# Squared relu of two MLPs: the square moved from VectorE to ScalarE

## The chip, the core and the metric

One core of a Trainium2 chip runs the whole kernel in one launch. The metric is the time of that launch on the device, in microseconds (us). Three timed runs of the kernel before gave 1197.14, 1199.34 and 1201.36 us; the median is 1199.34 us. The change is judged by the median of the changed kernel's runs against this.

## What is computed

A sequence of 256 tokens of width 1024 goes through two blocks, all in float32. The first block has two layers, each of attention and an MLP with a squared relu; the second has a SwiGLU layer, a hybrid mixer and a second SwiGLU layer, all three modulated by vectors that come from a condition. The change touches the two MLPs of the first block alone:

```python
D_MODEL, SEQ, D_FF = 1024, 256, 4 * 1024

def squared_relu_mlp(x, w_up, w_down):
    return jnp.square(jax.nn.relu(x @ w_up)) @ w_down

for layer in range(2):
    ...
    h = h + squared_relu_mlp(rms_norm(h, mlp_norm[layer]), w_up[layer], w_down[layer])
```

## The kernel before, in words

**Products in three parts.** Every float32 operand of a large product is split into a high part, rounded to the type fp32r, and a low part, the rest. Each product is three matmuls: high by high, high by low, low by high (`part`, lines 212 to 214, where tokens are the rows of the result; `by_feature`, lines 245 to 247, where features are). So every piece of a weight needs two instructions before TensorE can use it: ScalarE writes the high part `wh` (`prepare`, line 174, or line 178 where a gain is multiplied in) and VectorE the low part `wl` (line 175 or 179; for a few pieces GpSimd at line 175).

**Weights as a stream.** A list (`plan`) holds all pieces of 512 KB, called slabs, in the order of use. SyncE's queue loads them (line 147) into a ring of five buffers `raw` (RB = 5); a load can start when the slab five places ahead of it has been read by its last reader. The prepared parts lie in rings of five (WB = 5), freed by TensorE. `take` prepares up to two slabs beyond the one that is asked for. Between the slabs of the MLPs stand slabs of the modulation weights `w_ada`, about one for every two: these are not multiplied on TensorE, but by VectorE (`ada_step`, line 485, two instructions for a slab), and GpSimd adds the result up over the partitions (line 490) after every fourth slab.

**One MLP.** `hidden` runs over eight blocks of 512 hidden features (`MLP_CUTS`). For block j TensorE first makes the up product of block j (`by_feature`, 96 matmuls of 256 columns, into two tiles of PSUM), and then the down product of block j - 1 (`by_token`, 48 matmuls of 512 columns, accumulated in four tiles). I call these two an up pass and a down pass, and both together a round. Between the passes stands, in program order, the hidden part of block j (`up` in `mlp`, lines 836 to 840). It handles two tiles, and for each there are four instructions: ScalarE's relu (line 837, from PSUM), VectorE's product of relu and input (line 839, tile `sq`), ScalarE's high part `mh` of the square (line 259) and VectorE's low part `ml` (line 260). Their results are first used by TensorE one up pass later.

**Order.** The schedule is written by hand: each engine executes its instructions in the order in which the program lists them, and waits for semaphores where an operand comes from another engine. So a relu of the second tile stands on ScalarE's queue behind the high part of the first tile's square, which waits for VectorE. In the second MLP some rounds also hold VectorE instructions for the modulation (`modulation`, line 507), which wait for a small load of a gain row.

The tile `sq` is taken from a ring of six buffers (tag `rb`), the relu's tile from a ring of three (tag `ra`).

Of the kernel before, what the change touches and what calls it, by code (L numbers as in the profile page):

```python
# [12 lines left out]
AF = mybir.ActivationFunctionType  # L13
OP = mybir.AluOpType
# [14 lines left out]
def kernel(ctx: ExitStack, tc: tile.TileContext, a: dict, out: bass.AP):  # L29
    nc = tc.nc  # L30
    PE, ACT, DVE, POOL = nc.tensor, nc.scalar, nc.vector, nc.gpsimd
# [23 lines left out]
    def mm_ps(shape=(TP, 512)):  # L55
        return psm.tile(list(shape), F32, tag="mm", name="mm")
# [3 lines left out]
    def sb(tag, shape=(TP, 512), dt=F32, name=None):  # L60
        return s2.tile(list(shape), dt, tag=tag, name=name or tag, bufs=BUFS[tag])
# [4 lines left out]
    def tt(shape, name="t", dt=F32):  # L66
        return tiny.tile(list(shape), dt, tag="t", name=name)
# [7 lines left out]
    def cols(s):  # L75
        return slice(s * 512, (s + 1) * 512)
# [21 lines left out]
    def finish(*some):  # L98

        while any(s in sides for s in some):  # L100
            for s in some:
                if s in sides:
                    advance(s)
# [129 lines left out]
    def by_feature(idx, xT, ps, before=None):  # L233

        k = 0
        for i in idx:
            if before is not None:
                before(k)
            for wh, wl in take(i):
                xh, xl = (z[:, k % 4, :] for z in xT[k // 4])  # L240
                for n in range(2 * len(ps)):
                    c = slice(n * TP, (n + 1) * TP)
                    o = ps[n // 2][:, n % 2, :]

                    PE.matmul(o, lhsT=wh[:, c], rhs=xh, start=k == 0 and n % 2 == 0, stop=False)  # L245
                    PE.matmul(o, lhsT=wh[:, c], rhs=xl, start=False, stop=False)  # L246
                    PE.matmul(o, lhsT=wl[:, c], rhs=xh, start=False, stop=k == 7 and n % 2 == 1)  # L247
                k += 1
                if k % 2:
                    tick()  # L250
            done(i)
            tick()
# [33 lines left out]
    def hidden_part(q):  # L286

        hi, lo = pair("m", (TP, 2, S))
        split(hi, lo, q)
        return [(hi[:, j, :], lo[:, j, :]) for j in range(2)]  # L290
# [506 lines left out]
    def hidden(plans, cuts, up, update, order=None, tail=None):  # L797


        acc = [[None, None], [None, None]]  # L800
        made = None
        ups, downs = plans
        for j in range(len(cuts) + 1):
            new = up(j, ups[j]) if j < len(cuts) else None
            if j == 1:
                acc = [[acc_ps() for _ in range(2)] for _ in range(2)]
            if 0 < j < len(cuts):
                for s in range(2):
                    apart = tail is not None and j == len(cuts) - 1 and s == 1
                    by_token(downs[j - 1][s], by_block(made), [acc[t][s] for t in range(2)], first=j == 1,  # L810
                             last=(lambda t, n: t == 1 and n == len(downs[j - 1][s]) - 1) if apart else False)
            elif j == len(cuts):
                if tail is not None:
                    update(1, 1, acc[1][1])
                token_first(downs[j - 1], by_block(made), acc, False, lambda t, s: update(t, s, acc[t][s]),
                            order, tail)
            made = new

    def mlp(layer, plans, xT, vs, chains, next_chain, between=lambda j: None, order=BY_HALF):
        r2 = [None, None]  # L820

        def up(j, ids):
            between(j)
            ps = [mm_ps((TP, 2, S)) for _ in range(2)]

            def before(k):
                if j == 0:
                    finish(chains[0][k // 4], chains[1][k // 4])
            by_feature(ids[0], xT, ps, before)
            if j == 0:  # L830
                for t in range(2):
                    r2[t] = tt((TP, 1), "r2")
                    DVE.reciprocal(r2[t], vs[t][0])
            hT = []
            for p in ps:
                r = sb("ra", (TP, 2, S), name="relu")
                ACT.activation(out=r, in_=p, func=AF.Relu)
                q = sb("rb", (TP, 2, S), name="sq")
                DVE.tensor_tensor(q, r, p, op=OP.mult)
                hT += hidden_part(q)  # L840
            return hT

        def update(t, s, p):
            DVE.scalar_tensor_tensor(out=h[t][:, cols(s)], in0=p, scalar=r2[t], in1=h[t][:, cols(s)],
                                     op0=OP.mult, op1=OP.add)
            next_chain(t, s)
        hidden(plans, MLP_CUTS, up, update, order)
# [747 lines left out]
```

## Time and profile before

| what | value |
|---|---|
| timed runs | 1197.14, 1199.34, 1201.36 us; median 1199.34 us |
| the profiled execution | 1202.77 us, its span 1201.1 us |
| mean granted clock of TensorE | 0.991 |
| TensorE matmuls busy | 1163.7 us, 97% |
| VectorE busy | 847.7 us, 71% |
| ScalarE busy | 652.0 us, 54% |
| GpSimd busy | 301.3 us, 25% |
| read from memory | 240.65 MB, 201 GB/s over the span |
| the square on VectorE, line 839 | 32 instructions, 21.8 us |

The profile is of one execution, and all durations below come from it. Its own time is 1.67 us more than its span, and 3.43 us more than the median of the timed runs. Matmuls are pipelined, and the page models their ends: TensorE counts as busy from a matmul's start to its modelled end, so the idle time that a view gives is shorter than the delay between two starts. PE stands for TensorE's matmuls, PEld for its weight loads, DVE for VectorE, ACT for ScalarE, POOL for GpSimd, SP for SyncE; L839 is line 839.

### The profile page before, as it was taken

Reading aid. Unit: us, or ns where it says so; the run is one execution under the profiler, and the core shown is the slowest. Engines: PE = TensorE matmul, PEld = TensorE weight load, DVE = VectorE, ACT = ScalarE, POOL = GpSimd, SP = SyncE. Lnnn points to the kernel's source line nnn. Section 1 sums busy time; section 2 is a strip of 40 time slices with the busy share of each in tenths; the row PEclk is TensorE's granted clock in tenths of the full one; section 3 lists DMA queues with packets and bytes.
Section 4 is the critical chain, followed back from the end, with each engine's and each line's share of the span. In section 5 each row is a group of like instructions: output and inputs, shape, how many; then the busy total and the mean of one; then the engine's idle time right before and its main releaser. Section 6 shows DMA issues by size and latency. Waiting matters only on the chain.

```text
span 1201.1 us, 19954 instructions
## 1 busy us (share of the span) xinstructions
PE 1163.7 (97%) x7669; PEld 1051.3 (88%) x7669; DVE 847.7 (71%) x1188; ACT 652.0 (54%) x1115; POOL 301.3 (25%) x260
## 2 busy tenths in 40 slices
PE   8999999999999999999989999999999999999997
PEld 7987989988899799889868999979987887899996
DVE  5664688887676478788767888756776767666445
ACT  6476664555546664555654444545766563444443
POOL 3044202222002601112063121154147314112002
PEclk9999999999999999999989999999999999999999
DMA  8643567886653448789737888853733363877660
GB/s 274 188 140 107 178 218 253 282 272 215 193 171 119 137 147 277 244 283 308 252 121 248 298 278 303 292 163 101 222 90 104 104 225 110 272 222 244 209 192 36
DMA packets 128479, 243.04 MB, mean 202 GB/s; under 512 B 8515, under 2 KB 16612, under 8 KB 128384
## 3 DMA queue, kind: packets, MB, share of 16 engines
q1 hardware_dynamic: 126688, 239.96, 61.0%
q0 software_dynamic: 1376, 1.28, 0.5%
q8 instruction: 60, 0.98, 0.3%
q10 hardware_dynamic: 320, 0.53, 0.1%
q14 instruction: 35, 0.29, 0.1%
HBM read 240.65 MB, written 1.09 MB: 201 GB/s over the span
## 4 chain that ended last, share of the span: by engine, by line
PE 65%; DVE 16%; DMA 7%; ACT 6%; issue 4%; POOL 2%; SPq 0%; POOLq 0%; DVEq 0%; ACTq 0%
PE mm L247 8%; PE mm L246 8%; PE mm L245 8%; PE acc L212 8%; PE acc L213 7%; PE acc L214 7%; DVE wl L179 4%; DMA raw<-in_w_down_dram 4%; PE acc L245 3%; PE acc L247 3%; PE acc L246 3%; DVE wl L175 3%; ACT wh L174 2%; DVE ada L485 2%; PE mm L212 2%
## 5 line engine op out<-in xcount | busy, mean ns | idle before, releaser
L174 ACT CAST wh<-raw 128x1024 fp32r<-128x1024 f32 (+1 forms) x231 | 237.4, 1042 | 222.0 <-DMA raw<-in_w_down_dram 72.4
L175 DVE TENSOR_TENSOR wl<-raw,wh 128x1024 fp32r<-128x1024 f32 (+1 forms) x193 | 261.0, 1368 | 135.1 <-ACT wh L174 132.1
L247 PE MATMUL mm<-xh,wl 128*128 128x256 f32 x1088 | 308.6, 284 | 5.1 <-DVE wl L179 5.1
L245 PE MATMUL mm<-xh,wh 128*128 128x256 f32 x1088 | 308.5, 284 | 0.0
L246 PE MATMUL mm<-xl,wh 128*128 128x256 f32 x1088 | 307.8, 283 | 0.0
L179 DVE SCALAR_TENSOR_TENSOR wl<-raw,cols,wh 128x512 fp32r<-128x512 f32 (+1 forms) x270 | 204.1, 807 | 68.2 <-ACT wh L178 68.2
L247 PEld LDWEIGHTS mm<-xh,wl 128*128 128x128 f32 x1088 | 208.7, 192 | 6.4 <-DVE wl L179 6.3
L178 ACT ACTIVATE wh<-raw,cols 128x512 fp32r<-128x512 f32 (+1 forms) x270 | 175.9, 708 | 64.9 <-PE acc L246 20.4
L246 PEld LDWEIGHTS mm<-xl,wh 128*128 128x128 f32 x1088 | 208.7, 192 | 0.8
L245 PEld LDWEIGHTS mm<-xh,wh 128*128 128x128 f32 x1088 | 208.7, 192 | 0.8
L212 PE MATMUL acc<-wh,mh 128*128 128x512 f32 x524 | 207.4, 396 | 0.0
L213 PE MATMUL acc<-wl,mh 128*128 128x512 f32 x524 | 205.2, 392 | 0.5 <-DVE wl L175 0.5
L214 PE MATMUL acc<-wh,ml 128*128 128x512 f32 x524 | 205.0, 391 | 0.0
L490 POOL PARTITION_ALL_REDUCE ada<-ada x18 | 64.9, 3608 | 352.0 <-DVE ada L485 143.1
L175 POOL TENSOR_TENSOR wl<-raw,wh 128x1024 fp32r<-128x1024 f32 (+1 forms) x38 | 91.5, 2410 | 130.8 <-ACT wh L174 125.6
L214 PEld LDWEIGHTS acc<-wh,ml 128*128 128x128 f32 x524 | 98.8, 189 | 21.0
L212 PEld LDWEIGHTS acc<-wh,mh 128*128 128x128 f32 x524 | 98.9, 189 | 20.6 <-issue 1.6
L213 PEld LDWEIGHTS acc<-wl,mh 128*128 128x128 f32 x524 | 99.0, 189 | 20.1 <-DVE wl L175 1.1
L485 DVE SCALAR_TENSOR_TENSOR ada<-raw,c_act,ada 128x512 f32<-128x512 f32 x144 | 107.8, 749 | 2.8 <-DVE wl L175 0.3
L245 PE MATMUL acc<-xh,wh 128*128 128x256 f32 x352 | 101.9, 290 | 0.0
L247 PE MATMUL acc<-xh,wl 128*128 128x256 f32 x352 | 99.5, 283 | 0.0
L246 PE MATMUL acc<-xl,wh 128*128 128x256 f32 x352 | 99.5, 283 | 0.0
(318 smaller groups left out, 1634.4 us busy)
## 6 DMA issues: line engine op xcount, KB each, us to landing
raw<-in_w_ada_dram SPq DMA_DIRECT2D x72, 512.0 KB, 5.4
raw<-in_w_up_dram SPq DMA_DIRECT2D x64, 512.0 KB, 4.6
raw<-in_w_down_dram SPq DMA_DIRECT2D x64, 512.0 KB, 5.8
raw<-in_ffn_w_gate_dram SPq DMA_DIRECT2D x44, 512.0 KB, 4.6
raw<-in_ffn_w_up_dram SPq DMA_DIRECT2D x44, 512.0 KB, 4.6
raw<-in_ffn_w_down_dram SPq DMA_DIRECT2D x44, 512.0 KB, 5.3
raw<-in_moba_w_qkv_dram SPq DMA_DIRECT2D x23, 512.0 KB, 5.3
raw<-in_w_in_dram SPq DMA_DIRECT2D x20, 512.0 KB, 3.9
```

What stands on the lines that cost most here:

```text
L174: ACT.copy(hi, raw)
L175: (POOL if i in on_pool else DVE).tensor_tensor(lo, raw, f(hi), op=OP.subtract)
L178: ACT.mul(hi[:, k], raw[:, k], gain[k])
L179: DVE.scalar_tensor_tensor(out=lo[:, k], in0=raw[:, k], scalar=gain[k], in1=f(hi[:, k]), op0=OP.mult, op1=OP.subtract)
L212: PE.matmul(p, lhsT=xh, rhs=wh, start=first and n == 0, stop=False)
L213: PE.matmul(p, lhsT=xh, rhs=wl, start=False, stop=False)
L214: PE.matmul(p, lhsT=xl, rhs=wh, start=False, stop=last and n == len(ws) - 1)
L245: PE.matmul(o, lhsT=wh[:, c], rhs=xh, start=k == 0 and n % 2 == 0, stop=False)
L246: PE.matmul(o, lhsT=wh[:, c], rhs=xl, start=False, stop=False)
L247: PE.matmul(o, lhsT=wl[:, c], rhs=xh, start=False, stop=k == 7 and n % 2 == 1)
L485: DVE.scalar_tensor_tensor(out=acc, in0=raw[:, i, :], scalar=c_act[:, k:k + 1], in1=acc, op0=OP.mult, op1=OP.add)
L490: POOL.partition_all_reduce(acc, acc, TP, ReduceOp.add)
```

## The change

The square of the relu is no longer a product of the relu and its input on VectorE. ScalarE squares its own relu:

```diff
@@ -836,7 +836,7 @@
                 r = sb("ra", (TP, 2, S), name="relu")
                 ACT.activation(out=r, in_=p, func=AF.Relu)
                 q = sb("rb", (TP, 2, S), name="sq")
-                DVE.tensor_tensor(q, r, p, op=OP.mult)
+                ACT.activation(out=q, in_=r, func=AF.Square)
                 hT += hidden_part(q)
             return hT
```

`hidden_part` is as before: it makes `mh` on ScalarE and `ml` on VectorE.

## Rows read from the trace of the kernel before

**Rows 1.** Busy time by stage: both MLPs; columns are engines' busy us (instructions), clock, DMA.

```profile
148.20:303.40 155.20, 151.55 (x936) 136.47 (x935) 126.75 (x148) 84.87 (x125) 30.23 (x17) 1.00 0.73 244
454.30:613.60 159.30, 157.35 (x962) 141.09 (x961) 128.40 (x149) 86.50 (x129) 34.05 (x19) 1.00 0.81 269
```

**Rows 2.** Waits of PE from 115 to 320: total us, times, longest.

```profile
PE mm L247 <- DVE wl L179: 3.7, 5, 1.3
```

**Rows 3.** Waits of PE from 440 to 620.

```profile
PE mm L247 <- DVE wl L179: 1.4, 1, 1.4
...
PE acc L213 <- DVE wl L175: 0.5, 1, 0.5
```

**Rows 4.** Timeline of PE: start, duration; first matmuls of three down passes.

```profile
193.06 0.40 PE L212 MATMUL acc<-wh,mh 128*128 128x512 f32 x1
...
215.48 0.40 PE L212 MATMUL acc<-wh,mh 128*128 128x512 f32 x1
...
287.68 0.40 PE L212 MATMUL acc<-wh,mh 128*128 128x512 f32 x1
```

**Rows 5.** Chain that ended last, a round of the first MLP and the end: start, us, what.

```profile
211.80 5.84 DMA raw<-in_w_down_dram
...
218.83 1.23 DVE wl L175
220.06 0.61 DVE sq L839
...
220.69 0.63 ACT mh L259
...
223.32 0.69 DVE ml L260
...
277.74 0.39 PE mm L247
```

**Rows 6.** Timeline of ACT: the first relu of that round.

```profile
218.70 0.59 ACT L837 ACTIVATE relu<-mm 128x512 f32<-128x512 f32 x1
```

**Rows 7.** Groups by line: busy us, mean ns, then idle us before them and releaser.

```profile
L260 DVE TENSOR_TENSOR ml<-sq,mh 128x512 fp32r<-128x512 f32 x32 | 22.2, 693 | 22.0 <-ACT mh L259 22.0
L839 DVE TENSOR_TENSOR sq<-relu,mm 128x512 f32<-128x512 f32 x32 | 21.8, 681 | 1.4 <-ACT relu L837 1.4
...
L259 ACT CAST mh<-sq 128x512 fp32r<-128x512 f32 x32 | 19.9, 621 | 36.2 <-DVE sq L839 36.2
```

**Rows 8.** Instructions on the tile junk: ScalarE's square elsewhere; ns min/median/max.

```profile
L298 ACT ACTIVATE junk<-h x33: 416/632/634, 17.2 to 1195.0; 128x512 f32<-128x512 f32 x31, 128x256 f32<-128x256 f32 x2
```

**Rows 9.** Timeline of ACT in the mixer: a square of the tile just copied.

```profile
832.12 0.39 ACT L1177 COPY ckv<-acc 128x288 f32<-128x288 f32 x1
832.54 0.42 ACT L298 ACTIVATE junk<-ckv 128x256 f32<-128x256 f32 x1
```

**Rows 10.** Timeline in the second MLP: a hidden part behind a modulation's wait.

```profile
525.06 0.59 ACT L837 ACTIVATE relu<-mm 128x512 f32<-128x512 f32 x1
...
527.53 0.69 DVE L507 SCALAR_TENSOR_TENSOR mod<-mod,gn 128x512 f32<-128x512 f32 x1 [1.11 <-DMA gn<-in_norm_ffn_dram]
...
531.48 0.69 DVE L260 TENSOR_TENSOR ml<-sq,mh 128x512 fp32r<-128x512 f32 x1 [0.69 <-ACT mh L259]
```

**Rows 11.** Busy time from 196 to 198; columns as in the first group.

```profile
196.00:198.00 2.00, 2.00 (x10) 1.65 (x9) 1.31 (x3) 1.12 (x2) 0.00 (x0) 1.00 1.05 388
```

**Rows 12.** Timeline of PE: the first transpose behind the second MLP.

```profile
617.70 1.94 PE L265 MATMUL mm<-ident,hn 128*128 128x128 f32 x8 [4.08 <-DVE hn L980]
```

**Rows 13.** Timeline of ACT: table loads, and the squares that run behind them.

```profile
148.58 1.28 ACT L974 ACT_TABLE_LOAD   x1
...
302.30 0.63 ACT L298 ACTIVATE junk<-h 128x512 f32<-128x512 f32 x1 [2.12 <-DVE h L844]
...
562.48 1.28 ACT L322 ACT_TABLE_LOAD   x1
...
614.87 0.63 ACT L298 ACTIVATE junk<-h 128x512 f32<-128x512 f32 x1 [2.74 <-DVE h L844]
```

## The prediction

> **What bounds the kernel now.** I first read busy time by stage. In both MLPs TensorE is busy for all but a few microseconds at full clock, VectorE for four fifths of the time, ScalarE for just over half [rows 1]. So the question is not who is busiest but why TensorE ever stops there. The waits of PE answer it: in the first MLP five stops, 3.7 us in sum, all for a low weight part from VectorE [rows 2]; in the second two, 1.4 and 0.5 us, again for VectorE's weights [rows 3]. No wait for the hidden tiles is listed.
>
> Idle time understates a stop, because the matmul before it is still counted when nothing new starts. The starts of down passes show the true loss. An undisturbed round takes 215.48 - 193.06 = 22.42 us [rows 4]. The next three take 287.68 - 215.48 = 72.20 instead of 3 x 22.42 = 67.26 us: 4.94 us are lost, and all five stops lie there. That is (4.94 - 3.7) / 5 = 0.25 us a stop above its idle time. For the second MLP I take 1.4 + 0.5 + 2 x 0.25 = 2.4 us. **All that this change can win in the MLPs is therefore 4.94 + 2.4 = 7.3 us.**
>
> Last I read the chain of waits, to see what made the weights late. From 141 us to 277.74, where TensorE resumes after the last stop of the first MLP [rows 5], it holds no piece of TensorE. It goes round by round through the same stations: a load of w_down, ScalarE's cast, VectorE's low part, then the hidden part as product, cast, low part, and again for the second tile, then modulation steps and up weights, whose last read frees a buffer for the next load [rows 5]. Six hidden parts lie on it. So VectorE and ScalarE run a loop that is a little longer than TensorE's round, and fall behind until TensorE stops. In the round shown the first relu starts at 218.70 [rows 6], 3.2 us after TensorE had left for the down pass [rows 4].
>
> **The change, part by part.**
>
> Removed: 32 products on VectorE, 21.8 us [rows 7] (two MLPs x eight blocks x two tiles). ScalarE's casts sat idle 36.2 us for them [rows 7], 1.13 us for each; that wait goes too, because the cast now reads what its own engine wrote.
>
> Added: 32 squares on ScalarE. The nearest row is the same function on the same shape, with a sum beside it: 632 ns [rows 8]. Bounds: the relu of this shape takes 0.59 us [rows 6], the product it replaces 0.68 us [rows 7]; I take 0.63. The square reads a tile that its own engine has just written. The trace has such a pair: a copy from 832.12 lasting 0.39, and a square of that tile at 832.54 [rows 9], so 0.03 us between them. Sum: 32 x 0.63 = 20.2 us more on ScalarE.
>
> A weighing: here ScalarE's square (0.63 us) is no slower than VectorE's product (0.68 us) [rows 7, 8]. The Trainium skill, page "ScalarE: Activation LUTs", section "Rules for kernel authors", says to use VectorE, not ScalarE, for relu and mul, since VectorE is up to about three times faster per element in bf16. By that factor the square would be an estimated 3 x 0.68 = 2.0 us, the hidden part 6.6 us, and the change a loss of 2.0 us a block; the rows are in float32 and show no such gap.
>
> On the path: one hidden part. Before, from the first relu's start to the second low part's start: 223.32 - 218.70 = 4.62 us [rows 5, 6]. After, one tile on ScalarE is 0.59 + 0.03 + 0.63 + 0.03 + 0.62 = 1.90 us, two tiles 3.80, and the low part starts 0.02 later: 3.82 us. VectorE does not hold that up: its weight part ends at 220.06, 1.36 us after the relu's start, and the first cast only at 1.90. **Saving 0.80 us a block.** With the square at 0.59 it is 0.88, at 0.68 it is 0.70. It is less than product plus wait (1.3 us a tile), because VectorE now waits for ScalarE's longer string.
>
> First MLP: six blocks on the chain x 0.80 = 4.8 us by the last stop, against 4.94 lost; the first of the five stops, some 50 us earlier, already has four blocks ahead of it, 3.2 us. I leave 0.2 us standing.
>
> Second MLP, the 1.4 us stop: there VectorE waits at its modulation step until 527.53 while the relu started at 525.06 [rows 10]. Once the square is ScalarE's, both tiles' casts are done or nearly so when VectorE is free again. It issues two low parts from 528.14, the second about 0.6 later instead of at 531.48: 2.7 us saved against a stop of 1.65. The 0.5 us stop (0.75 true) has one block on its chain, 0.80: gone or almost; I leave 0.4 for both margins together.
>
> Costed at nothing, with their cover: ScalarE's 20.2 us, because the casts' 36.2 us of idle time stood in the same place in its queue; behind the squares stand only the weight casts, which now come 0.8 us earlier. The input tile in PSUM is released earlier, but nobody waits for it. The square's buffer is now written by ScalarE, so its release by a VectorE reader six tiles back needs a wait; that reader is three blocks old. No DMA is added; loads on SyncE's queue start earlier, as VectorE frees their buffers.
>
> Sum: 7.3 - 0.2 - 0.4 = 6.7 us. The profiled execution of 1202.77 would become 1196.1. That execution is 3.43 us above the median of 1199.34, and I take the saving as the same: **1192.6 us**. Bounds: all 7.3 us, and nothing at all if the margins fail.
>
> **The rivals.**
>
> Rival A, the loads refill the gap. The loop also holds a load of 5.84 us [rows 5]. If loads are limited by bandwidth and not by when a buffer comes free, the 0.8 us is given back while ScalarE waits for data. For it: in some stretches the DMA share is 1.05 at 388 GB/s [rows 11]. Against it: the mean over the MLP is 0.73 and 244 GB/s, and the second MLP runs at 269 [rows 1]; a round without stops needs only the same bytes in 22.42 instead of 24.07 us, 244 x 24.07 / 22.42 = 262 GB/s. Then only the second MLP gains, 2.4 us: 1196.9.
>
> Rival B, TensorE arrives earlier and waits longer. Behind the second MLP it stops for 4.08 us for a normalised tile [rows 12]. If what releases that stop keeps its own time, the gain is waited away there: 1199.3. Against it: that tile is made from the MLP's own output, so it moves along with TensorE; only work of other engines that is queued ahead of it and tied to loads could hold it back.
>
> Rival C, slower: the square needs another activation table. Two loads of 1.28 us [rows 13] a block make the hidden part 3.82 + 2.56 = 6.38, or 1.76 us longer than before. It decides from a square of 0.63 + 0.80 / 2 = 1.03 us on. Six blocks of the first MLP give 10.6 us, the second with its slack perhaps half of that: 1199.3 + 15.9 = 1215.2. Against it: squares run behind the load at 148.58 and behind that at 562.48 with no load of their own [rows 13], and relus run under the same tables. The same page, section "What ACT_TABLE_LOAD costs", gives about 2.66 us for a switch to another set, the drain included, and names relu, copy, identity and abs, not the square, as in every set; these rows speak against a switch.
>
> **How the numbers follow.** About 0.3% (3.6 us) is what a measurement of this kernel can tell from no change. My forecast has 0.58; A 0.20, of which 0.04 wins enough in the first MLP to pass 3.6 us; B 0.17; C and whatever else slows it 0.05. So faster is 0.58 + 0.04 = 0.62, same 0.16 + 0.17 = 0.33, slower 0.05. The forecast's own range is 1190.5 to 1195. The whole range starts at 1189.5 (all 7.3 us and the scatter of some 2 us that the three runs show) and ends at 1199.5, which takes in A and half of B: left out are half of B, C and a small tail below, under 0.2.
>
> **What would show it.** Right: no product on line 839 but 32 squares near 0.63 us, starting 0.03 us behind their relu; the casts' wait for VectorE gone; VectorE's wait for the casts, 22.0 us in sum [rows 7], up to some 28; the relu in the late rounds of the first MLP starting within about 3 us of TensorE's down pass; no stop for line 179 in either MLP; rounds of 22.42 us throughout. Wrong: stops for line 179 that stay although the hidden part is 0.8 us shorter (A); the stop before the transposes well over 4.08 us (B); table loads between relu and square (C).

## The result: 1193.73 us after, 1199.66 us before, and the profile after

Six runs of the changed kernel have a median of 1193.73 us (1191.97 to 1194.96), six of the kernel before 1199.66 us (1196.74 to 1201.36; three of these six are the runs that stood ahead of the prediction). The ratio is 0.9947 with a 95% interval of 0.9928 to 0.9967: the change wins 6.4 us of 1199.66, between 4.0 and 8.6. The forecast was 1192.6 us in a range of 1189.5 to 1199.5.

The profiled execution took 1193.64 us, its span is 1191.9 us. The page's busy times and its chain of waits (share of the span by engine):

```profile
PE 1160.6 (97%) x7669; PEld 1050.1 (88%) x7669; DVE 825.5 (69%) x1156; ACT 673.5 (57%) x1147; POOL 304.0 (26%) x260
...
PE 84%; DVE 6%; ACT 3%; POOL 2%; issue 2%; DMA 1%; SPq 0%; POOLq 0%; DVEq 0%; ACTq 0%
```

TensorE's busy share is 97% as before and tells nothing. VectorE has lost 22 us of work and ScalarE has won 21.5. The chain is what to look at: TensorE's part of it was 65% before and is 84% now, and VectorE's fell from 16% to 6%. The same line on the page of the kernel before:

```profile
PE 65%; DVE 16%; DMA 7%; ACT 6%; issue 4%; POOL 2%; SPq 0%; POOLq 0%; DVEq 0%; ACTq 0%
```

Before, the chain went through the MLPs by way of the weights; now it goes through them on TensorE.

The groups by line, which answer to [rows 7] (mean ns, then idle time in front):

```profile
L260 DVE TENSOR_TENSOR ml<-sq,mh 128x512 fp32r<-128x512 f32 x32 | 22.3, 697 | 30.6 <-ACT mh L259 30.6
L839 ACT ACTIVATE sq<-relu 128x512 f32<-128x512 f32 x32 | 20.2, 633 | 1.0
L259 ACT CAST mh<-sq 128x512 fp32r<-128x512 f32 x32 | 19.9, 621 | 1.0
```

The square costs 633 ns. The casts' wait for VectorE, 36.2 us before, has become 1.0 us in all, the 0.03 us between a square and its cast. VectorE's own wait for the casts grew from 22.0 to 30.6 us. By stage, the same lengths of the two MLPs as in [rows 1], each moved to where TensorE's first down pass of the stage starts:

```profile
146.87:302.07 155.20, 155.20 (x961) 140.31 (x960) 121.00 (x140) 97.99 (x146) 31.16 (x17) 1.00 0.77 255
448.05:607.35 159.30, 156.53 (x962) 141.06 (x961) 121.65 (x138) 97.77 (x147) 36.54 (x23) 1.00 0.82 272
```

In the first MLP TensorE has no idle time at all. (The second line ends inside the stop behind the MLP, which now starts earlier within a stretch of that length.) The loads run at 255 and 272 GB/s instead of 244 and 269. The granted clock is 1.00 in these stretches as it was in those of [rows 1], so it has no part in the difference. The list of TensorE's waits from 115 to 320 us is empty; that from 440 to 620 us holds only what stands behind the second MLP:

```profile
PE mm L265 <- DVE hn L980: 4.0, 1, 4.0
PE mm L212 <- ACT xh L259: 0.4, 1, 0.4
```

The first answers to [rows 12]: 4.04 us, as long as before. The starts of the first and the last of seven down passes in each MLP, on the timeline of PE:

```profile
146.89 0.40 PE L212 MATMUL acc<-wh,mh 128*128 128x512 f32 x1
...
281.41 0.40 PE L212 MATMUL acc<-wh,mh 128*128 128x512 f32 x1
...
448.11 0.40 PE L212 MATMUL acc<-wh,mh 128*128 128x512 f32 x1
...
582.63 0.40 PE L212 MATMUL acc<-wh,mh 128*128 128x512 f32 x1
```

Six rounds take 134.52 us in both, which is 6 x 22.42 to the last digit. Before, the same six rounds began and ended at these starts (the end of the first MLP's, 287.68, is in [rows 4]):

```profile
148.22 0.40 PE L212 MATMUL acc<-wh,mh 128*128 128x512 f32 x1
...
454.36 0.40 PE L212 MATMUL acc<-wh,mh 128*128 128x512 f32 x1
...
591.67 0.40 PE L212 MATMUL acc<-wh,mh 128*128 128x512 f32 x1
```

That is 139.46 us in the first MLP and 137.31 in the second: 4.94 and 2.79 us lost, 7.73 together. From here on "lost" means this: the length of these six rounds less 134.52 us.

**Where the time came from.** The two profiled executions differ by 9.2 us of span. Of these 7.73 lie in the two MLPs. Another 1.3 are already there when TensorE starts its first up pass (at 124.57 before, at 123.25 after), ahead of the first changed instruction; in the seven further kernels below the first pass compared starts between 145.94 and 147.35, where it was 148.22 before and is 146.89 after. That part is scatter of the executions, and one reason why the profiles differ by more than the medians, which are 5.93 us apart. It does not explain all of it: the profile of before is 3.1 us above its median, the profile after is at its own. So an execution at the median may well have lost less than 7.73 us in the MLPs; no profile of such a one was taken.

The hidden part whose like is in [rows 5, 6], on the timelines of ACT and DVE:

```profile
213.46 2.52 DVE L175 TENSOR_TENSOR wl<-raw,wh 128x1024 fp32r<-128x1024 f32 x2
214.62 0.59 ACT L837 ACTIVATE relu<-mm 128x512 f32<-128x512 f32 x1
215.25 0.63 ACT L839 ACTIVATE sq<-relu 128x512 f32<-128x512 f32 x1
215.91 0.62 ACT L259 CAST mh<-sq 128x512 fp32r<-128x512 f32 x1
216.44 0.59 ACT L837 ACTIVATE relu<-mm 128x512 f32<-128x512 f32 x1
216.56 0.69 DVE L260 TENSOR_TENSOR ml<-sq,mh 128x512 fp32r<-128x512 f32 x1 [0.58 <-ACT mh L259]
...
218.37 0.69 DVE L260 TENSOR_TENSOR ml<-sq,mh 128x512 fp32r<-128x512 f32 x1 [1.12 <-ACT mh L259]
218.98 1.53 DVE L485 SCALAR_TENSOR_TENSOR ada<-raw,c_act,ada 128x512 f32<-128x512 f32 x2
```

From the first relu's start to the second low part's are 218.37 - 214.62 = 3.75 us; the forecast had 3.82, and before it was 4.62. VectorE leaves the block, that is, starts its next instruction, 218.98 - 214.62 = 4.36 us after the relu. Before, it left it at 223.93, which is 5.23 us after the relu at 218.70 [rows 6]. The wait of the second low part, 1.12 us, is the price of the longer string on ScalarE; in a queue that is worked in order VectorE can do nothing else meanwhile.

Two further views of the kernel before, ACT and then DVE, show where the 0.87 us of difference sat:

```profile
220.69 0.62 ACT L259 CAST mh<-sq 128x512 fp32r<-128x512 f32 x1 [1.40 <-DVE sq L839]
221.22 0.59 ACT L837 ACTIVATE relu<-mm 128x512 f32<-128x512 f32 x1
222.67 0.62 ACT L259 CAST mh<-sq 128x512 fp32r<-128x512 f32 x1 [0.86 <-DVE sq L839]
...
223.93 1.53 DVE L485 SCALAR_TENSOR_TENSOR ada<-raw,c_act,ada 128x512 f32<-128x512 f32 x2
```

From the start of a tile's relu to the start of its cast were 220.69 - 218.70 = 1.99 us for the first tile and 222.67 - 221.22 = 1.45 for the second; after, 1.29 and 1.28. So 0.70 us were lost in the first tile, where the product stood on VectorE's queue behind a weight part until 220.06 [rows 5], and 0.17 in the second.

### The profile page after: what moved, and what is told of

Read it like the earlier page. It is cut to its first block, busy times and chain, and to the rows that moved or that the text cites. A ratio compares the mean times of both kernels' runs of the same rounds, so it can differ in the third digit from the quotient of the medians.

```text
span 1191.9 us, 19960 instructions
## 1 busy us (share of the span) xinstructions
PE 1160.6 (97%) x7669; PEld 1050.1 (88%) x7669; DVE 825.5 (69%) x1156; ACT 673.5 (57%) x1147; POOL 304.0 (26%) x260
## 3 DMA queue, kind: packets, MB, share of 16 engines
q0 software_dynamic: 1376, 1.28, 0.5%
## 4 chain that ended last, share of the span: by engine, by line
PE 84%; DVE 6%; ACT 3%; POOL 2%; issue 2%; DMA 1%; SPq 0%; POOLq 0%; DVEq 0%; ACTq 0%
PE mm L247 11%; PE mm L246 11%; PE mm L245 11%; PE acc L212 11%; PE acc L214 10%; PE acc L213 10%; PE acc L245 3%; PE acc L246 3%; PE acc L247 3%; PE mm L212 2%; PE mm L213 2%; PE mm L214 2%; PE mm L265 1%; POOL wl L175 1%; PE mm L638 1%
## 5 line engine op out<-in xcount | busy, mean ns | idle before, releaser
L175 DVE TENSOR_TENSOR wl<-raw,wh 128x1024 fp32r<-128x1024 f32 (+1 forms) x193 | 258.0, 1351 | 140.1 <-ACT wh L174 136.2
```

Source lines behind the costliest of these rows:

```text
L175: (POOL if i in on_pool else DVE).tensor_tensor(lo, raw, f(hi), op=OP.subtract)
```

## The experiments

Two theories. The **string theory** is the prediction's: what counts is how long the chain of hand-offs in one block keeps the engines from the next weights. The **load theory** is its rival: VectorE is simply relieved of 21.8 us of work, and it matters neither where nor how. All kernels were run beside the kernel before, whose medians on those chips were 1199.14 us (24 runs), 1199.07 (12) and 1199.25 (16).

### One MLP at a time

```diff
-                ACT.activation(out=q, in_=r, func=AF.Square)
+                if layer == 0:
+                    ACT.activation(out=q, in_=r, func=AF.Square)
+                else:
+                    DVE.tensor_tensor(q, r, p, op=OP.mult)
```

> ScalarE squares in the first MLP alone; the second keeps VectorE's product. String theory (the gain is the hidden part's shorter string of hand-offs between ScalarE and VectorE, 0.8 us a block, and shows only where TensorE stopped for weights): the first MLP's 4.9 us of stops go, the second's two stops (1.4 and 0.5 us idle) stay, so about 4.9 us faster than before. Load theory (the gain is the 21.8 us of work taken off VectorE, wherever it is taken): half of the gain, 3.0 us faster.

Measured: 1193.87 us, ratio 0.9961 (0.9948 to 0.9974), 4.7 us faster. The first MLP loses nothing. The second, with the old code, on the timeline of PE:

```profile
447.55 0.40 PE L212 MATMUL acc<-wh,mh 128*128 128x512 f32 x1
...
571.71 0.38 PE L247 MATMUL mm<-xh,wl 128*128 128x256 f32 x1 [0.29 <-DVE wl L179]
...
583.08 0.40 PE L212 MATMUL acc<-wh,mh 128*128 128x512 f32 x1
```

Its six rounds lost 135.53 - 134.52 = 1.01 us, not 2.79, with one stop of 0.29 us. So the second MLP's loss is not the same in every execution of the same code.

With `layer == 1` in the condition, the second MLP alone:

> ScalarE squares in the second MLP alone. String theory: the five stops of the first MLP stay (3.7 us idle, 4.9 us lost), the two of the second go: 2.4 to 2.8 us faster than before. Load theory: half of the gain, 3.0 us faster; the trace tells them apart by the stops, not the time.

Measured: 1196.84 us, ratio 0.9986 (0.9974 to 0.9999), 1.7 us faster, between 0.1 and 3.1. The second MLP loses nothing, and TensorE's waits in the first are back (total us, times, longest):

```profile
PE mm L247 <- DVE wl L179: 3.8, 5, 1.0
```

Six rounds of the first MLP take 139.89 us, 5.37 lost. The times alone hardly decide: half of the gain, 3.0 us, lies just outside the first interval (3.1 to 6.2 us) and just inside the second. In the first MLP the stops decide: there is none where ScalarE squares, and there are five where it does not. In the second they decide less, because the old code there lost 2.79 us in one execution and 1.01 in another.

### VectorE's work back, without anyone waiting for it

```diff
                 ACT.activation(out=q, in_=r, func=AF.Square)
-                hT += hidden_part(q)
+                hi, lo = pair("m", (TP, 2, S))
+                DVE.tensor_tensor(lo, r, p, op=OP.mult)
+                split(hi, lo, q)
+                hT += [(hi[:, j, :], lo[:, j, :]) for j in range(2)]
```

> ScalarE squares as in the change, but VectorE still makes its product as well, into the buffer of the low part, which the low part then overwrites; nobody waits for it, and VectorE would otherwise stand idle for the cast there. VectorE's work is that of before (21.8 us back), ScalarE's is that of the change. String theory: the second low part starts about 0.1 us later than in the change, so the gain stays, 5 to 6 us faster than before, with no stop of TensorE over 0.3 us in the MLPs. Load theory: the stops come back and the time is that of before, within 1 us.

Measured: 1191.83 us, ratio 0.9942 (0.9921 to 0.9963), 7.0 us faster than before (4.4 to 9.5), as fast as the change. The page's busy times show VectorE's work as before, 846.4 us:

```profile
PE 1159.7 (97%) x7669; PEld 1049.2 (88%) x7669; DVE 846.4 (71%) x1188; ACT 673.5 (57%) x1147; POOL 302.9 (25%) x260
```

And the block on the timeline:

```profile
214.71 0.59 ACT L837 ACTIVATE relu<-mm 128x512 f32<-128x512 f32 x1
...
215.99 0.68 DVE L841 TENSOR_TENSOR ml<-relu,mm 128x512 fp32r<-128x512 f32 x1
...
218.48 0.69 DVE L260 TENSOR_TENSOR ml<-sq,mh 128x512 fp32r<-128x512 f32 x1 [0.42 <-ACT mh L259]
219.09 1.53 DVE L485 SCALAR_TENSOR_TENSOR ada<-raw,c_act,ada 128x512 f32<-128x512 f32 x2
```

The products fill what were waits: the second low part's wait shrinks from 1.12 to 0.42 us, and VectorE leaves the block 4.38 us after the relu, as in the change. Neither MLP loses anything; the first and the last of the seven down passes in the first one, 134.51 us apart:

```profile
146.41 0.40 PE L212 MATMUL acc<-wh,mh 128*128 128x512 f32 x1
...
280.92 0.40 PE L212 MATMUL acc<-wh,mh 128*128 128x512 f32 x1
```

The load theory falls here: all the work is back, and all the gain is still there.

### The same work, behind the low parts

```diff
+            made = []
             for p in ps:
...
                 hT += hidden_part(q)
+                made.append((q, r, p))
+            for q, r, p in made:
+                DVE.tensor_tensor(q, r, p, op=OP.mult)
```

> The same instructions as the run in which VectorE makes its product as well, but both products of a block stand behind the two low parts instead of ahead of each, and write into the square's buffer when all its readers are done; nobody waits for them. ScalarE leaves the block as early as in the change. VectorE leaves it at 3.75 + 0.61 + 1.28 = 5.6 us after the first relu's start, where it was 5.2 before and 4.4 in the change. String theory in the form 'what counts is when VectorE gets back to the weights': six blocks x 0.4 = 2.5 us more stops than before in the first MLP, 2 to 4 us slower than before, although the work is that of a kernel 7 us faster. If what counts is when ScalarE gets back to its weight casts: the gain stays, 6 us faster than before.

Measured: 1201.26 us, ratio 1.0018 (1.0004 to 1.0032), 2.2 us slower than before, between 0.5 and 3.8. Timeline of the block (relu and the weight cast behind the block on ACT, the rest on DVE), and TensorE's waits in the first MLP:

```profile
218.09 0.58 ACT L838 ACTIVATE relu<-mm 128x512 f32<-128x512 f32 x1
...
221.71 2.56 ACT L178 ACTIVATE wh<-raw,cols 128x512 fp32r<-128x512 f32 x4
...
221.84 0.69 DVE L260 TENSOR_TENSOR ml<-sq,mh 128x512 fp32r<-128x512 f32 x1 [1.12 <-ACT mh L259]
222.45 1.28 DVE L844 TENSOR_TENSOR sq<-relu,mm 128x512 f32<-128x512 f32 x2
223.64 1.53 DVE L485 SCALAR_TENSOR_TENSOR ada<-raw,c_act,ada 128x512 f32<-128x512 f32 x2
```

```profile
PE mm L247 <- DVE wl L179: 4.8, 5, 1.7
```

VectorE leaves the block 223.64 - 218.09 = 5.55 us after the relu. Six rounds of the first MLP take 141.12 us, 6.60 lost. The same work in another order of VectorE's queue (only the buffer that the product writes differs) is worth 9 us: 1191.83 against 1201.26. No wait for the tiles in PSUM, which are now read later, stands in TensorE's list. ScalarE goes on to its next weight cast 221.71 - 218.09 = 3.62 us after the relu, as early as in the change (3.63), and that did not help, so it is VectorE's return to the weights that counts. The reverse, ScalarE alone kept longer, was not run.

### The product left on VectorE, the order changed

```diff
+            rs = []
             for p in ps:
                 r = sb("ra", (TP, 2, S), name="relu")
                 ACT.activation(out=r, in_=p, func=AF.Relu)
+                rs.append(r)
+            qs = []
+            for r, p in zip(rs, ps):
                 q = sb("rb", (TP, 2, S), name="sq")
                 DVE.tensor_tensor(q, r, p, op=OP.mult)
+                qs.append(q)
+            for q in qs:
                 hT += hidden_part(q)
```

> No square on ScalarE: the product stays on VectorE, and only the order changes: both relus, both products, then cast and low part of each tile. Work of both engines as before. String theory: with VectorE free 1.36 us after the first relu's start, the products end at 2.0 and 2.6, the casts at 2.7 and 3.3, and the second low part starts 3.3 us after the relu instead of 4.6: all stops go, 6 us faster than before, as the change or better by 0.5 at most. Load theory: no gain, the time of before within 1 us.

Measured: 1192.72 us, ratio 0.9950 (0.9932 to 0.9969), 6.0 us faster than before. Timeline of the block:

```profile
213.29 1.08 ACT L838 ACTIVATE relu<-mm 128x512 f32<-128x512 f32 x2
...
214.56 1.28 DVE L843 TENSOR_TENSOR sq<-relu,mm 128x512 f32<-128x512 f32 x2
215.27 1.22 ACT L259 CAST mh<-sq 128x512 fp32r<-128x512 f32 x2 [0.91 <-DVE sq L843]
215.92 1.29 DVE L260 TENSOR_TENSOR ml<-sq,mh 128x512 fp32r<-128x512 f32 x2
217.14 1.53 DVE L485 SCALAR_TENSOR_TENSOR ada<-raw,c_act,ada 128x512 f32<-128x512 f32 x2
```

No instruction has moved between engines, and the gain is that of the change. Taking the two tiles in pairs lets each engine work on one while the other has its neighbour, so each hand-off is paid once for both. VectorE leaves after 217.14 - 213.29 = 3.85 us. It is half a microsecond better than the change in the block and not better in the time, because neither has a stop left in an MLP to remove.

### ScalarE's string made longer

```diff
-                ACT.activation(out=q, in_=r, func=AF.Square)
+                for _ in range(2):
+                    ACT.activation(out=q, in_=r, func=AF.Square)
```

> The change with each square made twice, the second over the first: two more squares a block on ScalarE, 0.65 us each with the gap. VectorE's work is that of the change. String theory: the second low part starts 3.8 + 1.3 = 5.1 us after the first relu, 0.5 later than before, so the stops come back larger: six blocks x 0.5 = 3 us more in the first MLP and 1 to 3 more in the second, 4 to 6 us slower than before. Load theory (VectorE's load, ScalarE being idle for 45% of the span): no change against the changed kernel, 6 us faster than before.

Measured: 1202.71 us, ratio 1.0032 (1.0020 to 1.0043), 3.8 us slower than before, a little under what was expected. VectorE has less to do than in the kernel before. TensorE's waits in the first MLP, by the list of waits:

```profile
PE mm L247 <- DVE wl L179: 6.0, 8, 1.7
```

Six rounds of it take 142.75 us: 8.23 lost, 3.29 more than before where 3 were expected. The second MLP lost 1.53, less than before, and there the expectation was too high.

With `range(2 if p is ps[0] else 1)`, one square more a block:

> The change with the square of the first tile of each block made twice. String theory: the second low part starts 3.8 + 0.65 = 4.5 us after the first relu, 0.15 less than before: 0.9 us won in the first MLP, the long modulation wait of the second still covers it (1.7 us won there), so 2 to 3 us faster than before, and most stops of the first MLP are there again. Load theory: 6 us faster than before.

Measured: 1194.80 us, ratio 0.9966 (0.9952 to 0.9979), 4.1 us faster than before, more than expected, though the interval (2.5 to 5.7) reaches into the 2 to 3 us of the expectation. TensorE's waits in the first MLP:

```profile
PE mm L247 <- DVE wl L179: 3.2, 3, 1.2
```

Its first MLP lost 4.07, which is 0.87 less than before, where 0.9 was expected. The second lost nothing at all, though its string is only 0.2 us shorter: the expectation had left the smaller stop of 0.5 us standing.

### All together

| kernel | VectorE leaves the block, us after the first relu | lost, first MLP | lost, second MLP | median us |
|---|---|---|---|---|
| reordered | 3.85 | 0.00 | 0.00 | 1192.72 |
| the change | 4.36 | 0.00 | 0.00 | 1193.73 |
| product kept | 4.38 | 0.00 | 0.00 | 1191.83 |
| one square more | 5.02 | 4.07 | 0.00 | 1194.80 |
| before | 5.23 | 4.94 | 2.79 | 1199.66 |
| products behind | 5.55 | 6.60 | 2.37 | 1201.26 |
| each square twice | 5.69 | 8.23 | 1.53 | 1202.71 |

The second column is read in one block of the first MLP's middle. The second to sixth block of that MLP agree with it within 0.03 us, but for one late block in three of the kernels (5.48 before, 5.36 with the product kept, 4.37 reordered). From 5.02 to 5.69 us the first MLP loses (8.23 - 4.07) / 0.67 = 6.2 us more for each microsecond of a block, about the six blocks that lie on the chain; the two kernels in between lie 0.4 and 0.8 us under that line, so it is a rough one. The second MLP follows it less well. Three kernels besides the one before have VectorE's work of before (845.6 to 846.4 us busy against 847.7): reordered, product kept and products behind. They lie up to 9 us apart.

## Why the prediction was right

**The bound.** 4.94 us lost in the first MLP: all of it was won. 2.4 in the second: the profile of before lost 2.79, and all of it was won too. The added 0.25 us fits the stop of 1.4 us, whose round is 1.68 too long; the round with the stop of 0.5 us is 0.98 too long where 0.75 was taken, and 0.13 lie in a round without a listed stop. But the 2.79 is one execution's: with the old code there, another lost 1.01. The runs in which only the second MLP was changed gained 1.7 us with an interval of 0.1 to 3.1, which holds the 2.0 that the sum counted.

**The saving of 0.80 us a block.** Measured 0.87 (4.62 to 3.75). The difference is an overlap the sum left out: the second relu starts at 216.44, 0.09 before the first cast ends at 216.53. The terms stand: 0.63 for the square, 0.03 between a tile's instructions. The multiplication by six blocks is what the table shows, roughly.

**What was left standing.** 0.2 and 0.4 us; nothing stood. The sum's 6.7 us against 6.4 measured is agreement inside the interval of 4.0 to 8.6, which would hold the 7.73 us of the profiles as well. That the sum lies so close to the medians is partly luck: the margins that it left were not needed, and the saving read from a profile 3.43 us above the median was carried over to the median whole, which no run checks.

**The loop itself.** The prediction saw VectorE and ScalarE run a loop a little longer than TensorE's round. In two late rounds that is still so after the change. Timeline of ACT, the first relus of two blocks:

```profile
237.56 0.59 ACT L837 ACTIVATE relu<-mm 128x512 f32<-128x512 f32 x1
...
260.56 0.59 ACT L837 ACTIVATE relu<-mm 128x512 f32<-128x512 f32 x1
```

From 214.62 to the first of these are 22.94 us, from there to the second 23.00, against a round of 22.42. In these two rounds the hidden part still falls behind TensorE by half a microsecond each, but the MLP ends before TensorE has to stop. Whether a longer MLP would stop again was not run.

**The modulation's wait.** The forecast was two low parts in one go behind it, the second 0.6 us later. Timeline of DVE:

```profile
517.34 0.69 DVE L507 SCALAR_TENSOR_TENSOR mod<-mod,gn 128x512 f32<-128x512 f32 x1 [1.17 <-DMA gn<-in_norm_ffn_dram]
517.95 1.36 DVE L260 TENSOR_TENSOR ml<-sq,mh 128x512 fp32r<-128x512 f32 x2
519.22 1.53 DVE L485 SCALAR_TENSOR_TENSOR ada<-raw,c_act,ada 128x512 f32<-128x512 f32 x2
```

That is what happened; the wait for the gain row itself is still there, and VectorE is through 1.9 us after the step's start where it took 4.6 before (527.53 to 532.09).

**Rival A**, loads refill the gap: they did not, since TensorE has no stop left and its rounds last 22.42 us. ScalarE's waits don't show it. Its idle time in front of the casts of w_down between 120 and 320 us is 42.3 us before and 42.8 after, whatever ended it. What is put down to the loads fell from 39.6 to 22.4 us, but 13.9 are now put down to modulation steps of VectorE (line 485) and 3.0 to its weight parts. The 262 GB/s that the prediction worked out for rounds without stops were too many: it scaled the mean over the whole MLP, 244, which includes undisturbed rounds, by the length of the disturbed rounds alone. Over the stretch of [rows 1] the same bytes without the 4.94 us are 244 x 155.20 / 150.26 = 252 GB/s, and 255 were measured. **Rival B**: the stop behind the second MLP stayed at 4.04 us and moved along. **Rival C**: no table load stands between a relu and its square, and the squares start 0.03 to 0.04 us behind. The late relus of the first MLP, forecast within about 3 us of TensorE's down pass, start at 237.56 and 260.56, 1.0 and 1.6 us after the passes' starts at 236.57 and 258.99. One sign was missed: VectorE's wait for the casts was to grow to some 28 us and grew to 30.6.

**The page's rule.** The rule of the Trainium skill, page "ScalarE: Activation LUTs", section "Rules for kernel authors", to keep relu and mul off ScalarE, did not decide here: 633 ns against 681 is almost the same price, and the run that leaves the product on VectorE and changes the order alone is as fast.

**Where the reason was too narrow.** The shorter string holds, but the prediction tied it to the engine that squares. The order of the two tiles does as much. It also measured the string to the start of the second low part. With the products behind, that start comes 221.84 - 218.09 = 3.75 us after the relu, as in the change, and the kernel is slower than before: what counts is when VectorE goes on to the weights.

## What to carry to other kernels

When an engine waits for a neighbour in the middle of its queue, count the time until it returns to the work that the bound engine needs, not its busy time: here the same work in two orders was 9 us apart, and 21.8 us of added work that fell into waits cost nothing. Read the loss from the length of equal rounds rather than from idle time, and follow the chain of waits back to see how many such blocks lie on it; the product of the two, up to the loss itself, was the gain in the first MLP. Before an operation is moved to another engine, try issuing two tiles side by side, which hides the hand-offs of each behind the other.

## What was not expected

The second MLP's loss doesn't come from its own code alone: with that code unchanged it was 2.79 us in the profile of before, but 1.01 where only the first MLP had been changed. One profile of each doesn't tell whether a first MLP that ends without delay also helps the second, or whether it is scatter of the loads; that stays open.

The hand-offs themselves were not slow. In the block after, the low part starts at 216.56, 0.03 us behind the cast that ends at 216.53 on the other engine: the same step as between two dependent instructions on ScalarE. What the change took away is the product's turn in VectorE's queue behind other work.
